# Linear attention on one core: the third pair's load of Q in pieces of 112, 10, 3 and 3 partitions, with three tiny loads between them

## The chip, the cores and the metric

The kernel runs on one core of a Trainium2 chip. The metric is the device time of one execution in microseconds (us); lower is better. Quoted for the kernel before is the median of three runs, 126.63 us (126.56 to 127.84).

## The reference

Inputs Q, K and V have the shape (8, 12, 512, 64) in float32: 96 heads of 512 rows with 64 columns. Linear attention without a mask is computed for each head:

```python
Q_feat = np.maximum(0, Q) + 1
K_feat = np.maximum(0, K) + 1
KV = np.einsum('bhkd,bhkv->bhdv', K_feat, V)
K_sum = np.sum(K_feat, axis=2)
numerator = np.einsum('bhqd,bhdv->bhqv', Q_feat, KV)
denominator = np.einsum('bhqd,bhd->bhq', Q_feat, K_sum)
return (numerator / (denominator[:, :, :, None] + 1e-10)).astype(np.float32)
```

Each of the four arrays has 12.58 MB, so 37.75 MB are read and 12.58 MB written.

## The kernel before

The 96 heads are worked on in 12 groups of eight heads (`NG` = 12), and two groups make a pair; there are six pairs, numbered 0 to 5 here, so the third is pair 2. All loads of a pair are issued together by `load_pair`: K, V and Q, each one transfer of 128 partitions, 2 MB in HBM, cast to bf16 on the way (1 MB in SBUF). They go through GpSimd's DMA queue (POOL), lines L115 (K and V) and L121 (Q). For pair 0 they are smaller pieces, and half of its Q comes through SyncE's queue (SP, L93). In a load of Q, one partition holds two runs of 32 rows of 64 columns: 16 KB of float32. Raw tiles have two buffers, so pair s+2's K can be loaded only when pair s's features have been read.

For each group the steps are:

- `k_features` and `q_features` (VectorE, L146): max(x + 1, 1) in bf16.
- `v_blocks` (VectorE L164, ScalarE L162): V of four heads is copied into a block layout `v_all` with a column of ones per block.
- `keys_values` (TensorE, L180): KV and K_sum accumulate in PSUM; ScalarE writes them to `kva_all` (L190, L191).
- `transposes` (TensorE L201, copies L204): the features of Q, transposed.
- `out_matmuls` and `norms` (TensorE L214, VectorE L231 and L232): numerator and denominator, then reciprocal and product into `o_sb`, which has three buffers.
- `store` (POOL L135 for the first ten groups, SP L138 and L141 for the last two): 1 MB of float32 to HBM.

The order on every engine is the order of the program (`manual_schedule`); each engine's queue is in order, and the framework adds the semaphores. POOL's queue holds, in this order: the loads of pairs 0, 1 and 2; then, for each later pair, K, V, Q and two stores; then the rest of the stores. The main loop issues pair 2's loads at the end of group 1, and pair 3's at the end of group 3:

```python
            if g % 2 and g // 2 + 2 < NG // 2:
                load_pair(g // 2 + 2)
            if g >= LAG:
                store(g - LAG)
```

For GpSimd's transfers the framework has eight completion semaphores, used in turn, so a transfer also waits until the eighth one before it has landed, unless that is known already. A transfer that waits holds up everything behind it in POOL's queue.

Of the kernel before, what the change touches and what calls it, by code (L numbers as in the profile page):

```python
# [8 lines left out]
FP32 = mybir.dt.float32  # L9
# [4 lines left out]
IN_BUFS = 2  # L14
OUT_BUFS = 3
LAG = 3


@with_exitstack
def kernel(  # L20
# [19 lines left out]
    nc = tc.nc  # L40

    B, H, S, D = Q.shape
    P = 128
# [10 lines left out]
    def view(t, c):  # L54
        return t.flatten_outer_dims().rearrange("(n p c) d -> p n c d", p=P, c=c)

    q_eights = view(Q, C4)
# [13 lines left out]
    psum = ctx.enter_context(tc.tile_pool(name="psum", bufs=2, space=bass.MemoryType.PSUM))  # L71
    psum_qt = ctx.enter_context(tc.tile_pool(name="psum_qt", bufs=2, space=bass.MemoryType.PSUM))

    identity = const.tile([P, P], BF16, name="identity")
    NV = 4
    v_all = const.tile([P, 2, 2, C2, 4 * D1], BF16, name="v_all")
# [7 lines left out]
    bufs = {}  # L84
# [33 lines left out]

    def load_q(s):
        t = in_pool.tile([P, 2, C4, D], BF16, name="q_raw")  # L120
        nc.gpsimd.dma_start(out=t, in_=q_eights[:, 2 * s : 2 * s + 2])  # L121
        rows = t.rearrange("p n (r c) d -> p n r c d", c=C)
        for e in range(2):
            raw["q", 2 * s + e] = [rows[:, n, :, 4 * e : 4 * e + 4] for n in range(2)]

    def load_pair(s):
        load("k", (2 * s, 2 * s + 1))
        load("v", (2 * s, 2 * s + 1))
        load_q(s)

    def store(g):
        s = g // 2
        o_to = o_dram[:, 2 * NP * s : 2 * NP * s + 2 * NP]
        if g < NG - 2:
            nc.gpsimd.dma_start(out=o_to[:, g % 2 : 2 * NP : 2], in_=outs[s][:, g % 2 : 2 * NP : 2])  # L135
            return
        if g == NG - 2:
            nc.sync.dma_start(out=o_to[:, 0 : 2 * NP : 2], in_=outs[s][:, 0 : 2 * NP : 2])  # L138
            return
        for h in range(2):  # L140
            nc.sync.dma_start(  # L141
                out=o_to[:, 2 * h + g % 2 : 2 * NP : NP], in_=outs[s][:, 2 * h + g % 2 : 2 * NP : NP]
            )
# [6 lines left out]
    def k_features(g):  # L150
        k_raw = raw.pop(("k", g))
        kf = kf_pool.tile([P, C2, 2, D], BF16, name="kf")
        for n in range(2):
            feature(kf[:, :, n], k_raw[:, n])
        kfs[g] = kf
# [12 lines left out]
    def q_features(g):  # L168
        q_raw = raw.pop(("q", g))
        qf = qf_pool.tile([P, R, C // 2, 2, D], BF16, name="qf")  # L170
        for n in range(2):
            feature(qf[:, :, :, n], q_raw[n])
        qfs[g] = qf

    def keys_values(g):
        kf = kfs.pop(g)
        kva_ps = psum_kva.tile([P, 4 * D1], FP32, name="kva_ps")
        for c in range(C2):
            for n in range(2):
                nc.tensor.matmul(  # L180
                    kva_ps[64 * n : 64 * n + 64],
                    lhsT=kf[:, c, n, :],
                    rhs=v_all[:, g % 2, n, c, :],
                    start=(c == 0),
                    stop=(c == C2 - 1),
                )
        kva = kva_diag[g % NV]
        for n in range(2):
            ps = slice(64 * n, 64 * n + 64)
            nc.scalar.copy(out=kva[ps, :, n, 0:D], in_=kva_ps[ps, 0 : 4 * D].rearrange("p (b d) -> p b d", b=4))  # L190
            nc.scalar.copy(out=kva[ps, :, n, D], in_=kva_ps[ps, 4 * D : 4 * D1])  # L191
# [49 lines left out]
    def output(g):  # L241
        for h in range(2):
            out_matmuls(g, h)
            norms(g, h)
# [11 lines left out]
    with tc.manual_schedule():  # L256
# [18 lines left out]
        for g in range(last - 1):  # L275
# [12 lines left out]
# [4 lines that stand above are left out]
        k_features(last - 1)  # L292
# [5 lines left out]
        keys_values(last - 1)  # L298
        store(last - 1 - LAG)
        q_features(last - 1)  # L300
# [8 lines left out]
        output(last)  # L309
        for g in range(last - LAG, NG):  # L310
            store(g)
# [30 lines left out]
```

## Time and profile before

| | us |
|---|---|
| median of three runs | 126.63 |
| the profiled execution's own time | 126.47 |
| its span, first to last instruction | 124.7 |
| VectorE (DVE) busy | 90.1 (72%) |
| TensorE (PE) busy | 64.2 (52%) |
| ScalarE (ACT) busy | 59.6 (48%) |
| GpSimd (POOL) busy | 26.1 (21%) |
| HBM read and written | 404 GB/s over the span |

Busy times are those of compute engines and of GpSimd's work on issuing transfers. The page also cuts the span into 40 slices of 3.1 us: a digit is the busy share of a slice in tenths, and the DMA row is the mean over the 16 DMA engines. A line of a timeline begins with the start and the duration in us; brackets at its end hold the idle time before it and what ended that. "k_raw<-in_K_dram" is a transfer from K in HBM into the tile `k_raw`.

Two kinds of records in the trace stand behind the page: packets (start, duration, size and queue of each piece that a DMA engine moves) and landings (the time of each of the 16 rises of a transfer's semaphore). They don't name the DMA engine.

### The profile page before, as it was taken

To read this page: it belongs to the slowest core of one execution; us is meant where nothing else is said; L and a number is where in the kernel's file an instruction comes from. 1 tells how busy PE (TensorE), PEld (TensorE's weight loads), DVE (VectorE), ACT (ScalarE), POOL (GpSimd) and SP (SyncE) were. 2 spreads that over 40 slices of the span, in tenths; PEclk is the share of its full clock that TensorE was granted. 3 is DMA by queue.
4 is the path that set the end of the run, shared out by engine and by line. 5 is a ranking of instruction groups with operands and counts; after the bars stand their busy time and mean duration, and the time that the engine had idled before them with its cause. 6 is when DMAs were issued, how large, how long until landed. Compare 5 with 4: busy or idle time off the path is not lost.

```text
span 124.7 us, 2349 instructions
## 1 busy us (share of the span) xinstructions
PE 64.2 (52%) x960; PEld 52.6 (42%) x960; DVE 90.1 (72%) x190; ACT 59.6 (48%) x86; POOL 26.1 (21%) x53
## 2 busy tenths in 40 slices
PE   0000874600596837939099690069394369874200
PEld 0000654600475826829088490058183158663000
DVE  4875735206999989998999950799958799969700
ACT  7505169806009981398803981603982283650000
POOL 6992020400001460207202070302020200020000
PEclk9999999995559996799855999657999855999655
DMA  3999999999999999999999999999999999999993
GB/s 89 320 212 216 206 211 212 212 215 218 206 212 212 220 213 206 212 215 217 230 406 327 210 212 219 212 342 395 230 202 215 219 247 417 419 417 415 406 409 135
DMA packets 11819, 32.13 MB, mean 258 GB/s; under 512 B 544, under 2 KB 544, under 8 KB 11680
## 3 DMA queue, kind: packets, MB, share of 16 engines
q0 software_dynamic: 10592, 28.84, 97.5%
q1 hardware_dynamic: 1216, 3.15, 6.7%
q8 instruction: 7, 0.11, 0.3%
q14 instruction: 4, 0.03, 0.1%
HBM read 37.75 MB, written 12.58 MB: 404 GB/s over the span
## 4 chain that ended last, share of the span: by engine, by line
DMA 51%; DVE 19%; PE 10%; ACT 7%; POOL 6%; issue 2%; DVEq 0%; ACTq 0%; POOLq 0%
DMA v_raw<-in_V_dram 51%; DVE o_sb L232 7%; PE kva_ps L180 7%; DVE v_all L164 7%; ACT qt L204 3%; ACT v_all L162 3%; POOL kva_all L271 2%; POOL k_raw L115 2%; DVE recip L231 2%; PE qt_ps L201 1%; PE o_ps L214 1%; POOL v_raw L115 1%; DVE qf L146 1%; DVE qt L204 1%; DVE kf L146 1%
## 5 line engine op out<-in xcount | busy, mean ns | idle before, releaser
L180 PE MATMUL kva_ps<-v_all,kf 128*64 128x260 bf16 x384 | 33.0, 343 | 16.8 <-DVE v_all L164 15.5
L214 PE MATMUL o_ps<-kva_all,qt 128*64 128x130 bf16 x384 | 19.7, 237 | 34.2 <-DVE recip L231 25.9
L164 DVE COPY v_all<-v_raw 32x2048 bf16<-32x2048 bf16 x36 | 26.1, 725 | 15.0 <-DMA v_raw<-in_V_dram 14.6
L180 PEld LDWEIGHTS <-kf 128*64 128x64 bf16 x384 | 26.6, 140 | 20.4 <-DVE v_all L164 15.9
L232 DVE TENSOR_TENSOR o_sb<-o_ps,recip 128x512 f32<-128x512 f32 x48 | 33.2, 692 | 1.6
L162 ACT COPY v_all<-v_raw 32x2048 bf16<-32x2048 bf16 x12 | 22.6, 1893 | 18.2 <-DMA v_raw<-in_V_dram 18.0
L214 PEld LDWEIGHTS <-qt 128*64 128x64 bf16 x384 | 13.7, 116 | 39.1 <-issue 23.2
L190 ACT CAST kva_all<-kva_ps 64x256 bf16<-64x256 f32 x24 | 8.9, 370 | 30.7 <-PE kva_ps L180 30.6
L204 ACT COPY qt<-qt_ps 128x1024 bf16<-128x1024 bf16 x23 | 22.2, 1015 | 2.2 <-PE qt_ps L201 1.7
L201 PE MATMUL qt_ps<-identity,qf 128*128 128x128 bf16 x192 | 14.8, 236 | 1.3 <-ACT qt L204 1.1
L135 POOL DMA_DIRECT2D out_dram<-o_sb x10 | 8.3, 830 | 32.1 <-DVE o_sb L232 27.3
L146 DVE TENSOR_SCALAR kf<-k_raw 128x1024 bf16<-128x1024 bf16 x24 | 9.5, 436 | 7.0 <-DMA k_raw<-in_K_dram 7.0
L201 PEld LDWEIGHTS <-qf 128*128 128x128 bf16 x192 | 12.6, 107 | 4.1 <-issue 1.8
L115 POOL DMA_DIRECT2D k_raw<-in_K_dram x7 | 5.4, 765 | 34.4 <-DVE kf L146 34.0
L231 DVE RECIPROCAL recip<-o_ps 128x8 f32<-128x8 f32 x48 | 9.6, 200 | 1.5 <-PE o_ps L214 1.2
L115 POOL DMA_DIRECT2D v_raw<-in_V_dram x7 | 5.4, 772 | 17.4 <-ACT v_all L162 17.4
L146 DVE TENSOR_SCALAR qf<-q_raw 128x1024 bf16<-128x1024 bf16 x22 | 8.2, 432 | 0.0
L249 DVE MEMSET v_all<- 128x2600 f32 x2 | 4.5, 2225 | 1.1 <-issue 1.1
L191 ACT CAST kva_all<-kva_ps 64x4 bf16<-64x4 f32 x24 | 4.1, 169 | 0.0
L121 POOL DMA_DIRECT2D q_raw<-in_Q_dram x5 | 3.5, 705 | 0.0
L250 ACT COPY v_all<-zero 128x1560 f32<-128x1560 f32 x2 | 2.9, 1488 | 0.0
L271 POOL MEMSET kva_all<- 128x130 bf16 x16 | 2.4, 196 | 0.0
(14 smaller groups left out, 6.6 us busy)
## 6 DMA issues: line engine op xcount, KB each, us to landing
out_dram<-o_sb POOLq DMA_DIRECT2D x10, 1024.0 KB, 25.2
k_raw<-in_K_dram POOLq DMA_DIRECT2D x5, 1024.0 KB, 21.7
v_raw<-in_V_dram POOLq DMA_DIRECT2D x5, 1024.0 KB, 21.8
q_raw<-in_Q_dram POOLq DMA_DIRECT2D x5, 1024.0 KB, 25.9
q_first<-in_Q_dram SPq DMA_DIRECT2D x1, 1024.0 KB, 4.9
k_raw<-in_K_dram POOLq DMA_DIRECT2D x2, 512.0 KB, 9.7
v_raw<-in_V_dram POOLq DMA_DIRECT2D x2, 512.0 KB, 11.4
out_dram<-o_sb SPq DMA_DIRECT2D x1, 1024.0 KB, 7.0
```

The lines of the kernel that those rows point to most:

```text
L115: nc.gpsimd.dma_start(out=bufs[x, s][:, ms], in_=drams[x][:, of])
L135: nc.gpsimd.dma_start(out=o_to[:, g % 2 : 2 * NP : 2], in_=outs[s][:, g % 2 : 2 * NP : 2])
L146: nc.vector.tensor_scalar(out=dst, in0=src, scalar1=1.0, scalar2=1.0, op0=ALU.add, op1=ALU.max)
L162: nc.scalar.copy(out=v_all[ps, g % 2, :, :, b * D : b * D + D], in_=v_raw[ps])
L164: nc.vector.tensor_copy(out=v_all[ps, g % 2, :, :, b * D : b * D + D], in_=v_raw[ps])
L180: nc.tensor.matmul(kva_ps[64 * n : 64 * n + 64], lhsT=kf[:, c, n, :], rhs=v_all[:, g % 2, n, c, :], start=(c == 0), stop=(c == C2 - 1),)
L190: nc.scalar.copy(out=kva[ps, :, n, 0:D], in_=kva_ps[ps, 0 : 4 * D].rearrange("p (b d) -> p b d", b=4))
L201: nc.tensor.transpose(qt_ps[:, c, r], qf[:, r, 2 * half + c, :, :], identity)
L204: copy(out=qts[g // 2][:, lo : lo + 2], in_=qt_ps.rearrange("p c r q -> p c q r"))
L214: nc.tensor.matmul(ops[c // 4][64 * j : 64 * j + 64, c // 2 % 2, (c % 2) * W : (c % 2) * W + W], lhsT=qt[:, c, q : q + 16, :], rhs=kva[:, ...
L231: nc.vector.reciprocal(out=recip, in_=cells[:, :, :, :, D:D1])
L232: nc.vector.tensor_tensor(out=o_sb[:, 2 * h + g % 2 : 2 * NP : NP, 4 * i : 4 * i + 4].rearrange("p n (b c) d -> p b c n d", b=2), in0=cell ...
```

## The change

Only `load_q` for pair 2 differs. Its one transfer of 128 partitions becomes four, of 112, 10, 3 and 3 partitions, which fill the same tile in order. Between them, three tiny transfers of 6, 4 and 6 partitions read two runs of 64 bytes per partition from the same part of Q into small float32 tiles of their own; nothing reads these tiles. All seven go through GpSimd's queue, in the order of `PIECES`. The bytes that the kernel needs and all compute instructions are the same.

```diff
+SPLIT = 2
+PIECES = ((112, True), (10, True), (6, False), (3, True), (4, False), (3, True), (6, False))
...
+    skip_pool = ctx.enter_context(tc.tile_pool(name="skip_pool", bufs=1))
+    skips = []
...
     def load_q(s):
         t = in_pool.tile([P, 2, C4, D], BF16, name="q_raw")
-        nc.gpsimd.dma_start(out=t, in_=q_eights[:, 2 * s : 2 * s + 2])
+        if s == SPLIT:
+            lo = 0
+            for n, real in PIECES:
+                if real:
+                    nc.gpsimd.dma_start(
+                        out=t[lo : lo + n], in_=q_eights[lo : lo + n, 2 * s : 2 * s + 2]
+                    )
+                    lo += n
+                else:
+                    skip = skip_pool.tile([8, 2, 16], FP32, name=f"skip{len(skips)}")
+                    skips.append(skip)
+                    nc.gpsimd.dma_start(
+                        out=skip[0:n], in_=q_eights[0:n, 2 * s : 2 * s + 2, 0, 0:16]
+                    )
+            assert lo == P
+        else:
+            nc.gpsimd.dma_start(out=t, in_=q_eights[:, 2 * s : 2 * s + 2])
```

## The prediction

> **What bounds the kernel now.** I read the page from the top: the 40 slices, the DMA queues, the chain that ended last. Then came POOL's waits, POOL's and VectorE's timelines around the change, and last the landing records of the trace (each transfer raises its semaphore 16 times, once per DMA engine).
>
> The page, slices, queues, chain:
>
> ```profile
> PE   0000874600596837939099690069394369874200
> DVE  4875735206999989998999950799958799969700
> DMA  3999999999999999999999999999999999999993
> GB/s 89 320 212 216 206 211 212 212 215 218 206 212 212 220 213 206 212 215 217 230 406 327 210 212 219 212 342 395 230 202 215 219 247 417 419 417 415 406 409 135
> ...
> q0 software_dynamic: 10592, 28.84, 97.5%
> q8 instruction: 7, 0.11, 0.3%
> q14 instruction: 4, 0.03, 0.1%
> ...
> DMA 51%; DVE 19%; PE 10%; ACT 7%; POOL 6%; issue 2%; DVEq 0%; ACTq 0%; POOLq 0%
> ```
>
> The DMA row is at 9 from the second slice to the last but one, while PE and DVE have holes. GB/s counts bytes written: near 212 is a load that reads float32 and writes bf16, near 415 a store. From slice 33 (102 us) on there are stores alone, still at full rate. So what sets the end is how many bytes each of the 16 DMA engines has to move, and which engine finishes last. The chain view ends in DVE's last multiply, but that store finds a queue in front of it: the last store is issued at 117.6 us and lands at 123.81.
>
> The landing records say how even the 16 are. For the last store they are 122.10, 122.11, 122.28, 122.64, 122.67, 122.86, then 123.09, 123.19, 123.24, 123.25, then 123.32, 123.33, 123.34, 123.35, 123.46 and 123.81. The mean is 123.00: the last engine is 0.81 us behind it. The spread is not there at the start: the second load of V lands within 0.56 us (17.65 to 18.21). It grows by one engine at a time after each 16 KB packet of the instruction queue q8 (25.9, 44.7, 55.6 us and so on, 0.9 us each): at 28 us one engine is 0.84 behind the next, at 62 us three are. So engines that also carry instructions are late, and stay late.
>
> POOL's timeline and waits, where the third pair (pair 2) and the next are issued:
>
> ```profile
> 22.54 0.70 POOL L121 DMA_DIRECT2D q_raw<-in_Q_dram  x1
> 37.10 0.77 POOL L115 DMA_DIRECT2D k_raw<-in_K_dram  x1 [13.86 <-DVE kf L146]
> 42.36 0.82 POOL L115 DMA_DIRECT2D v_raw<-in_V_dram  x1 [4.49 <-ACT v_all L162]
> 43.17 0.70 POOL L121 DMA_DIRECT2D q_raw<-in_Q_dram  x1
> 43.85 1.80 POOL L135 DMA_DIRECT2D out_dram<-o_sb  x2
> 51.94 0.75 POOL L115 DMA_DIRECT2D k_raw<-in_K_dram  x1 [6.28 <-DVE kf L146]
> ```
>
> The first line is the transfer that is cut up. It is issued at 22.54 and lands at 48.86: 26 us in the queue. POOL itself idles 13.86 us before its next transfer.
>
> **The change, part by part.**
>
> *One load becomes four; rows move between engines.* 128 rows on 16 engines are 8 each. A row of pair 2's Q is 16 KB of float32; V before it lands at 42.74 on the mean of the engines and Q at 47.72, so 8 rows take 4.98 us and one row 0.62. In the change 112 rows give 7 to each engine, if spread evenly, and 16 rows in pieces of 10, 3 and 3 are left, which no longer fall one on each engine. Where they fall the trace can't show, since it has no transfer of fewer than 128 rows; so bounds. Best: the six engines that are early at the end get two of these rows, the four in the middle one, the six late ones none. The early end at 122.86 + 0.62 = 123.48 at the latest, the middle at 123.25, the late at 123.81 - 0.62 = 123.19; the end moves from 123.81 to 123.48, or -0.33. Worst: the latest engine itself has one row more (+0.62), or two more (+1.23). Two readings can be counted out, engines numbered 0 to 15. If each small transfer begins at the engine where the last one stopped, one row each, the pieces fall on 0-9, 0-2 and 7-9 and the tiny loads on the gaps: 6 engines get an extra row, 4 none, and 6 lose one. If each begins at the same engine, three engines get two extra rows. I take the first and its best end, because 6, 4 and 6 are also the groups of the sorted landings; the order of the engines within them is taken on trust.
>
> The Trainium skill (DMA: Bandwidth & Descriptors, "Why a DMA increments its semaphore by 16 and not by 1") states the first reading for GpSimd transfers whose count has no larger share: k consecutive engines from a cursor that moves on. It also has an exception, measured for some direct copies, in which the rows fill the engines from 0. The sum is -0.33 by the one and up to +1.23 by the other; no run here shows either yet.
>
> *Six more transfers in the queue.* Each ends in one 4-byte semaphore packet on every engine, 22 ns in the packet records: 6 x 22 = +0.13 us on each engine, all of it on the bound. They could be had for 9 ns (the records' least): +0.05.
>
> *The tiny loads.* 6 + 4 + 6 rows with two runs of 64 bytes are 32 packets, two per engine if spread. The nearest rows are the 4-byte packet (9 to 22 ns) below and the 2 KB packet of a store (84 ns) above: 0.02 to 0.17 us. 64 bytes are nearer to 4: I take 0.05. A page of the skill speaks against all of this (same page, "Measured", its rule and fit): a GpSimd DMA has about 2.0 us fixed, and transfers under 64 KB are mostly overhead. The trace disagrees for queued transfers: landings are 4.9 to 5.0 us apart for one load after another, which is the packets' own time (a load of K is 32 packets per engine, 154 ns apart: 4.93). By the rule six transfers would be +12 us; by the row they are the +0.13 above.
>
> *POOL's time.* Six more issues at 0.70 us (the Q line above; the smallest, for half the bytes, is 0.57) are 4.2 us. They fall into the 13.86 us of idle before the next K, so nothing; without that cover it would be 4.2 us of later issues, and again only as far as the queue runs out.
>
> *New waits on POOL.* In the built program a GpSimd transfer waits for the eighth one before it, and six small ones bring this closer. The first three-row piece waits for pair 1's K (landed 23.16), the skip of 4 for its V (29.03), the second three-row piece for its Q (33.89), the last skip for pair 2's K (38.84). All are queued before the 112 rows are through (about 48). Behind them stands pair 3: K now waits for pair 2's V, 43.84 instead of 37.10; V for the 112 rows, about 48.2 instead of 42.36; Q and two stores follow until about 51.5, and the next K is issued at 51.94 anyway. Does the queue run dry? The earliest engine is through pair 2's Q at 47.24 in the old trace. From issue to first packet the trace gives only an upper bound: the very first K is issued at 1.29 and starts at 4.93, behind the first Q, so at most 3.64. 43.9 + 3.64 = 47.5 is 0.3 us past that engine, which in the change is one with more rows, through at 47.9. For V: 48.2 + 3.64 = 51.8, before K is through (52.2). So nothing, and at the bound 0.3.
>
> *VectorE* now waits for four semaphores before the Q features of pair 2. They start late anyway:
>
> ```profile
> 48.94 0.69 DVE L232 TENSOR_TENSOR o_sb<-o_ps,recip 128x512 f32<-128x512 f32 x1
> 49.55 0.75 DVE L146 TENSOR_SCALAR qf<-q_raw 128x1024 bf16<-128x1024 bf16 x2
> ```
>
> 49.55 against a landing at 48.86: 0.69 us of cover. Without it a late row would push DVE, the transposes and the stores of that pair, which wait in the same deep queue.
>
> **The sum.** Against the profiled execution: 126.47 us, of which 124.70 are span and 1.77 lie around it. -0.33 + 0.13 + 0.05 = -0.15, so 126.32. The median of the three runs is 126.63, 0.16 above the profiled execution; -0.15 from it is 126.48, and I say 126.5.
>
> **The rivals.**
>
> *The rows fall on the wrong engines* (the slower side). Place: the engine that lands last at 123.81. Price: +0.62 for one row more, +1.23 for two, and 0.18 for packets: 127.4 or 128.0. It decides as soon as the latest engine has nine rows; over 1% it is only with ten. For it: the trace names no engine. Against it: the counts 6, 4, 6. Chance 0.16.
>
> *The rows spread evenly*, the pieces being cut over all 16 engines: then nothing is balanced and only packets are left, 126.63 + 0.18 = 126.8. Against it: three rows are six runs, which 16 engines can't share evenly. Chance 0.12.
>
> *The queue runs dry* behind POOL's later waits. Place: pair 3's K, with 3.3 us between its issue and the end of pair 2's Q instead of 10. Price: each us it starts past 47.9 is a us at the end. At the bound for the start 0.3: 126.8; if the tiny loads land late, some 2 us and 128.5. For it: POOL has no idle left there. Against it: every wait has landed before the 112 rows. Chance 0.07.
>
> *More than balancing*: perfect balance gives 123.00, -0.81, so 126.0 with the packets. Over 1% faster needs a gain that no row shows. Chance 0.10, half of it over 1%.
>
> **How the numbers follow.** The forecast keeps 0.55; its own range is 126.2 (markers free) to 126.9 (upper prices of the tiny loads and of a 0.3 us gap). Within 1% (125.4 to 127.9), about what a measurement of this kernel can tell from no change, lie the forecast, the even spread, one row too many and most of the balanced case. Slower by over 1%: two rows on the latest engine (about half of the first rival) and the dry queue, with some room for a price that I missed: 0.17. Faster by over 1%: 0.08. The range to hold it 8 times in 10 goes from full balance to one row on the wrong engine: 125.9 to 127.6.
>
> **What would show it.** Right: the last store's landings lie within 1.0 us instead of 1.71, the last near 123.7; pair 3's K is issued near 44 and V near 48; the DMA row stays at 9; the Q features of pair 2 still start near 49.5. Wrong: one engine lands over 0.5 us behind the next at the end (wrong rows), a slice near 48 to 54 us drops below 9 (dry queue), or the spread is unchanged (no rows moved). A time beyond 127.6 or below 125.9 means that a step of the sum is missing.

## The result and the profile after

| | before | after |
|---|---|---|
| median, us | 126.55 (6 runs) | 128.03 (6 runs) |
| the profiled execution's own time, us | 126.47 | 128.83 |
| span, us | 124.7 | 127.0 |
| last landing of the last store, mean of the 16 engines, us | 123.00 | 124.30 |
| the same, last engine, us | 123.81 | 126.14 |

The ratio is 1.0113 (95% interval 1.0075 to 1.0151): the change makes the kernel slower, by 1.5 us of 126.6. The prediction was 126.5 with a range of 125.9 to 127.6, so it was wrong in size and in sign. (The slowest of the six runs is left out of the ratio: its state differs from the others'.)

In all 14 profiles of this case the execution's own time is 2.65 to 2.69 us more than the last landing of the last store. So two things make up the time: when the 16 engines are through on the mean (1.30 us later after the change), and how far the last engine is behind that mean (0.81 us before, 1.84 after).

The page after. Again the DMA and GB/s rows in 40 slices, the queues, and the chain:

```profile
DMA  3999999999999999999999999999999999999991
GB/s 88 328 209 213 210 208 211 217 209 217 208 211 213 221 186 170 197 213 221 219 408 323 197 210 216 219 341 388 228 214 213 217 294 414 418 417 412 406 353 62
...
q0 software_dynamic: 10800, 28.84, 96.5%
...
DMA 56%; DVE 20%; ACT 7%; PE 7%; issue 2%; POOL 1%; ACTq 0%; POOLq 0%
```

The DMA row is still at 9, so by that row nothing happened. The row below tells it: slices 15 to 17 (44 to 54 us) move 186, 170 and 197 GB/s where the kernel before moved 213, 206 and 212. Packets became longer there (an example follows below) and count as busy for all of their length, so the share stays up while the bytes fall.

The same as a table by stretches: busy time of each engine, then PE's clock, DMA share and GB/s. First two stretches of before, then after:

```profile
core 0: us, PE busy (x) PEld busy (x) DVE busy (x) ACT busy (x) POOL busy (x), PEclk, DMA share, GB/s
47.00:50.00 3.00, 2.41 (x32) 2.01 (x34) 2.90 (x9) 0.16 (x1) 0.00 (x0) 0.66 1.08 205
50.00:53.00 3.00, 3.00 (x46) 2.46 (x44) 2.99 (x7) 1.11 (x5) 0.75 (x1) 0.78 1.12 210
```

```profile
44.00:47.00 3.00, 0.27 (x9) 0.23 (x7) 2.87 (x7) 2.50 (x5) 1.16 (x1) 0.89 1.05 209
47.00:50.00 3.00, 2.90 (x38) 2.37 (x36) 2.52 (x6) 0.00 (x0) 1.18 (x2) 0.54 1.03 159
50.00:53.00 3.00, 2.37 (x48) 1.90 (x42) 2.99 (x8) 2.12 (x6) 2.48 (x4) 1.00 1.10 190
53.00:56.00 3.00, 0.42 (x8) 0.28 (x8) 2.89 (x6) 2.58 (x2) 0.38 (x2) 1.00 1.12 210
```

The missing bytes, (205 - 159) x 3 + (210 - 190) x 3 = 198 KB, are 0.93 us at 212 GB/s. The landings say the same. On the mean of the 16 engines, pair 3's K lands 9.93 us after pair 2's V before and 11.02 us after, and pair 3's Q 19.85 and 21.06 us after that V. What a kernel takes longer than 19.85 us for this last stretch is called its loss below: 1.21 us for the changed kernel, -0.01 in a second profile of the kernel before.

What happens there is seen in POOL's timeline (start, duration, then the transfer; in brackets the idle time and what ended it):

```profile
22.53 1.27 POOL L129 DMA_DIRECT2D q_raw<-in_Q_dram  x2
23.79 0.57 POOL L136 DMA_DIRECT2D skip<-in_Q_dram  x1
24.34 0.57 POOL L129 DMA_DIRECT2D q_raw<-in_Q_dram  x1
28.95 0.60 POOL L136 DMA_DIRECT2D skip<-in_Q_dram  x1 [4.04 <-DMA v_raw<-in_V_dram]
33.84 0.55 POOL L129 DMA_DIRECT2D q_raw<-in_Q_dram  x1 [4.28 <-DMA q_raw<-in_Q_dram]
38.80 0.55 POOL L136 DMA_DIRECT2D skip<-in_Q_dram  x1 [4.41 <-DMA k_raw<-in_K_dram]
44.05 1.16 POOL L119 DMA_DIRECT2D k_raw<-in_K_dram  x1 [4.70 <-DMA v_raw<-in_V_dram]
48.82 0.76 POOL L119 DMA_DIRECT2D v_raw<-in_V_dram  x1 [3.61 <-DVE recip L251]
```

The last three of the seven pieces and tiny loads each wait for the eighth transfer before, one landing after another, and so do the next two loads: pair 3's K is issued at 44.05 instead of 37.10, its V at 48.82 instead of 42.36. (The last line names DVE; the eighth transfer before that V is the piece of 112 rows, which lands at 48.24.) The first packets of that K start at 47.16 us, right behind pair 2's Q, so no gap shows at first sight. But between 47.3 and 47.8 us six packets of K last 1.09 to 1.23 us, where the same packet in a running queue lasts 0.17. That the engines had nothing read ahead is how I read this; the records don't show the reading side.

### The profile page after: what moved, and what is told of

It is laid out like the page before. It is cut to its first block, busy times and chain, and to the rows that moved or that the text cites. A ratio compares the mean times of both kernels' runs of the same rounds, so it can differ in the third digit from the quotient of the medians.

```text
span 127.0 us, 2358 instructions
## 1 busy us (share of the span) xinstructions
PE 65.8 (52%) x960; PEld 53.9 (42%) x960; DVE 89.8 (71%) x190; ACT 59.6 (47%) x86; POOL 30.2 (24%) x59
## 4 chain that ended last, share of the span: by engine, by line
DMA 56%; DVE 20%; ACT 7%; PE 7%; issue 2%; POOL 1%; ACTq 0%; POOLq 0%
DMA v_raw<-in_V_dram 56%; DVE v_all L184 8%; DVE o_sb L252 8%; PE kva_ps L200 6%; ACT qt L224 3%; ACT v_all L182 3%; DVE recip L251 2%; ACT kva_all L210 1%; DVE qf L166 1%; DVE qt L224 1%; POOL k_raw L119 1%; DVE kf L166 1%; PE o_ps L234 1%; PE qt_ps L221 0%; ACT kva_all L211 0%
## 5 line engine op out<-in xcount | busy, mean ns | idle before, releaser
L184 DVE COPY v_all<-v_raw 32x2048 bf16<-32x2048 bf16 x36 | 25.4, 707 | 15.5 <-DMA v_raw<-in_V_dram 15.1
L221 PE MATMUL qt_ps<-identity,qf 128*128 128x128 bf16 x192 | 16.2, 249 | 0.7 <-ACT qt L224 0.4
L221 PEld LDWEIGHTS <-qf 128*128 128x128 bf16 x192 | 13.7, 113 | 3.4 <-issue 1.4
L136 POOL DMA_DIRECT2D skip<-in_Q_dram x3 | 1.7, 574 | 8.4 <-DMA k_raw<-in_K_dram 4.4
L129 POOL DMA_DIRECT2D q_raw<-in_Q_dram x4 | 2.4, 599 | 4.3 <-DMA q_raw<-in_Q_dram 4.3
```

What stands on the lines that cost most here:

```text
L184: nc.vector.tensor_copy(out=v_all[ps, g % 2, :, :, b * D : b * D + D], in_=v_raw[ps])
L221: nc.tensor.transpose(qt_ps[:, c, r], qf[:, r, 2 * half + c, :, :], identity)
```

## The experiments

Three theories. **W**: the later issue of pair 3's loads lets the DMA queue run dry, fully or nearly. **P**: each small transfer has a price of its own on every engine (the landings of the small transfers of the changed kernel are 0.18 to 0.20 us apart). **R**: the rows went to engines that were late anyway (the last landings of the changed kernel spread over 3.31 us instead of 1.71).

### More and more tiny loads, no row moved

Pair 2's Q stays whole; 4, 5, 6 or 8 tiny loads of 16 partitions follow it (the list is written short here). The number decides what pair 3's K must wait for.

```diff
-PIECES = ((112, True), (10, True), (6, False), (3, True), (4, False), (3, True), (6, False))
+PIECES = ((128, True),) + ((16, False),) * n      # n = 4, 5, 6, 8
```

n = 4: 

> Pair 2's Q is one transfer of 128 partitions again, followed by four tiny loads of 16 partitions each. No row moves, and with four extra transfers pair 3's K waits for pair 1's Q (landed 34), so it is still issued at about 37. Theory W (the later waits on POOL let the DMA queue run dry): no loss, mean landing as before within 0.15 us, time within 0.3 us of before. Theory P (each small transfer costs about 0.19 us on every engine, as the landings of the changed kernel are apart): mean of the landings up by 4 x 0.19 = 0.76, time +0.7 us. Theory R (only the rows on wrong engines cost): no loss.

n = 5: 

> Pair 2's Q whole, then five tiny loads of 16 partitions: pair 3's K waits for pair 2's K, issued near 39.5, V near 44.4, Q near 49. Theory W: all of these are still more than 4 us ahead of the queue's end, so no loss between 47 and 53 us, time 126.5 to 127.1. If the loss grows with the number of transfers: between the kernel with four (126.95) and the one with six (128.85), about 127.9.

n = 6: 

> The same with six tiny loads of 16 partitions: no row moves, but pair 3's K now waits for pair 2's V and is issued at about 44, V at about 48, as in the changed kernel. Theory W: pair 3's K starts cold, its first packets on the early engines take about 1.1 us, the engines lose about 0.6 to 0.9 us between 47 and 53 us, time +0.7 to +1.0 us. Theory P: 6 x 0.19 = +1.1 us, only 0.4 more than with four. Theory R: within 0.3 us of before.

n = 8: 

> Pair 2's Q whole, then eight tiny loads of 16 partitions. The last tiny load now waits for that Q (landed at about 48.5), and pair 3's K for the first tiny load, so K is issued near 50, when the queue is empty. Theory W: first packet about 3.1 us after the issue and about 1 us more until it runs at rate, so all engines stand still from 48.5 to about 53: 4 to 5.5 us lost on each engine, time 130.5 to 132.5. If instead six or more extra transfers have some fixed price: about 129.

| n | issue of pair 3's K, of its V, us | loss, us | median, us | ratio (interval) |
|---|---|---|---|---|
| before | 37.1, 42.4 | 0 | 126.6 | |
| 4 | 37.2, 41.6 | 0.06 | 126.95 | 1.0024 (1.0009 to 1.0038) |
| 5 | 39.6, 44.6 | 0.33 | 126.99 | 1.0029 (1.0001 to 1.0057) |
| 6 | 44.7, 50.3 | 1.38 | 128.85 | 1.0180 (1.0143 to 1.0217) |
| 8 | 49.8, 50.7 | 5.88 | 132.74 | 1.0470 (1.0428 to 1.0512) |

The issues with n = 5, then with n = 6 (the first of these lines names DVE; the transfer that K waits for, pair 2's K, lands at 39.01):

```profile
39.56 0.79 POOL L119 DMA_DIRECT2D k_raw<-in_K_dram  x1 [4.72 <-DVE recip L251]
44.59 1.13 POOL L119 DMA_DIRECT2D v_raw<-in_V_dram  x1 [4.24 <-ACT qt L224]
```

```profile
44.74 1.16 POOL L119 DMA_DIRECT2D k_raw<-in_K_dram  x1 [4.73 <-DMA v_raw<-in_V_dram]
50.26 0.92 POOL L119 DMA_DIRECT2D v_raw<-in_V_dram  x1 [4.36 <-DMA q_raw<-in_Q_dram]
```

The steps are not those of a price per transfer: in the median the fifth costs nothing and the sixth about 1.9 us, as W says. W had the place right but priced it low: 0.7 to 1.0 us were expected for n = 6, and it is 2.3; for n = 8 132.74 us is just above the 132.5 expected at most. The landings of the tiny loads are 0.18 to 0.19 us apart here too, yet with four of them pair 3's K lands 5.00 us after pair 2's Q, against 4.95 before: a small transfer delays its own semaphore, hardly the bytes behind it. P falls. The 0.3 to 0.4 us of n = 4 and n = 5 are in part unevenness: the mean of the last landings is 123.04 and 123.15, against 123.00 and 123.07 in two profiles of the kernel before, but the last engine is 1.23 and 1.01 us behind that mean, against 0.81 and 1.23. Whether the extra transfers make this is not shown. The spread of the last landings is 3.11 us with n = 6, though no row was moved: a wide spread is no sign of R.

With eight the queue is empty, and the page shows what a start costs. Its DMA and GB/s rows, and POOL's timeline:

```profile
DMA  3999999999999953999999999999999999999991
GB/s 105 302 212 212 211 209 210 212 217 210 212 213 214 217 101 27 194 212 214 210 197 412 280 212 212 220 239 413 294 213 214 214 236 402 421 416 415 406 398 76
```

```profile
49.27 0.51 POOL L136 DMA_DIRECT2D skip<-in_Q_dram  x1 [4.34 <-DMA skip<-in_Q_dram]
49.78 0.89 POOL L119 DMA_DIRECT2D k_raw<-in_K_dram  x1
50.67 0.86 POOL L119 DMA_DIRECT2D v_raw<-in_V_dram  x1
```

K is issued at 49.78 and its first packet starts at 51.38. From 52.5 to 53.0 us the queue moves 131 GB/s, from 53.0 to 53.5 it moves 205. From issue to full rate that is about 3.2 us.

### The same waits and transfers, even rows

```diff
+PIECES = ((112, True), (16, True)) + ((16, False),) * 5
```

> 112 partitions, the other 16 in one piece, five tiny loads of 16: the same seven transfers and the same waits on POOL as in the changed kernel (K at 44, V at 48.8), but each engine has eight rows. Theory W: the dry queue is there, 0.7 to 1.0 us lost on each engine between 47 and 53 us, time 127.5 to 128.3. Theory R: 126.6 to 126.9.

128.96 us, ratio 1.0171 (1.0130 to 1.0211), loss 1.72 us. The rows are even and the whole slowdown is there, more of it than the 128.3 expected at most. R is not needed for it.

### The same rows, without the late issue

The third tiny load is moved behind pair 3's Q:

```diff
+PIECES = ((112, True), (10, True), (6, False), (3, True), (4, False), (3, True))
...
+            if s == SPLIT + 1:
+                skip = skip_pool.tile([16, 2, 16], FP32, name="skip_last")
+                nc.gpsimd.dma_start(out=skip[0:6], in_=q_eights[0:6, 2 * s : 2 * s + 2, 0, 0:16])
```

> The four pieces and the first two tiny loads as in the changed kernel, so the rows lie the same; the third tiny load is issued behind pair 3's Q. With five extra transfers ahead of it, pair 3's K waits for pair 2's K (39) and V for pair 2's V (44.4) instead of 44 and 48.8. Theory W (POOL's late issue lets the DMA queue run dry): the loss between 47 and 53 us is gone (under 0.1 us an engine), mean of the last landings within 0.3 us of before, time 126.3 to 127.2. Theory R (the rows): spread of the last landings about 3.3 us as in the changed kernel, time 127.3 or more. If the rows balance as intended and W holds: spread under 1.3 us, 126.2.

POOL's timeline of this kernel:

```profile
39.45 0.78 POOL L119 DMA_DIRECT2D k_raw<-in_K_dram  x1 [4.68 <-DVE recip L254]
44.47 1.14 POOL L119 DMA_DIRECT2D v_raw<-in_V_dram  x1 [4.24 <-DMA v_raw<-in_V_dram]
49.13 0.70 POOL L141 DMA_DIRECT2D q_raw<-in_Q_dram  x1 [3.53 <-DMA q_raw<-in_Q_dram]
```

127.09 us, ratio 1.0030 (1.0005 to 1.0054), loss 0.21. One tiny load moved by three places takes back about 1 us of the 1.5. The last landings spread over 2.06 us. Five extra transfers with whole rows, which are issued at the same times, have the ratio 1.0029: against them the rows, as they lie in the change, show no cost, and against the kernel before at most the 0.5 us. They gain nothing.

### Where the rows fall

> The pieces of 112, 10, 3 and 3 partitions without the tiny loads: three extra transfers, no later issue of pair 3's K. If small transfers go on at the engine where the last one stopped, 10 + 3 + 3 cover the 16 engines once and the rows are even: last landings spread by 1.7 us as before, time +0.1 (W, R) or +0.5 us (P). If each small transfer begins at the same engine, three engines get two rows more: spread 2.5 us or more, time +0.6 to +1.2 us.

> Pieces of 112 and 10, a tiny load of 6, a piece of 6: three extra transfers, no later issue of pair 3's K. If transfers go on where the last one stopped, six engines get one row more, six one less, four none, as in the changed kernel though not all the same engines. Theory R: spread of the last landings 2.3 to 3.3 us and time +0.4 to +1.2 us if the rows go to engines that are late, less than 1.3 us and -0.3 if they go to early ones. Theories W and P: spread near 1.7 us; W time within 0.3 us of before, P +0.5 us.

> The mirror of the kernel with a 6-partition piece behind a tiny load of 6: 112, tiny 6, 10, tiny 10, 6. If small transfers go on where the last one stopped, the six engines that lost a row there get one here. Four extra transfers, no later issue of pair 3's K. If the late engines are a fixed set and rows matter, one of the two mirrors is slower than before and the other not: the sum of their differences to before is near zero, each within 0.6 us. Theory W alone: both within 0.3 us of before.

```diff
+PIECES = ((112, True), (10, True), (3, True), (3, True))                              # first
+PIECES = ((112, True), (10, True), (6, False), (6, True))                             # second
+PIECES = ((112, True), (6, False), (10, True), (10, False), (6, True))                # third
```

126.68 us, ratio 1.0000 (0.9979 to 1.0021); 126.79 us, 1.0025 (0.9999 to 1.0051); 127.16 us, 1.0041 (1.0023 to 1.0060). None loses anything in the queue (0.04, 0.04, 0.05 us). The first keeps the engines nearly as they were: the standard deviation of their landings goes from 0.52 us (pair 2's V) to 0.64 (pair 3's K); with five tiny loads and whole rows it goes from 0.37 to 0.45. In the second it goes from 0.58 to 0.72, in the third from 0.39 to 0.73, and in the kernel of the section before from 0.33 to 0.62, with groups near -0.7, -0.35 and +0.4 us and one engine at +1.63. The third and the last fit the reading that a small transfer goes on at the engine where the last one stopped; the second, which should show it too, hardly does (rows that fall on early engines would hide it). The Trainium skill (DMA: Bandwidth & Descriptors, "Why a DMA increments its semaphore by 16 and not by 1") states that a GpSimd transfer of k shares, with k under 16, takes k consecutive engines from a round-robin cursor. The records name no engine, so this stays open. The spreads of the last landings are 2.43, 3.28 and 2.83 us, and no run shows what the rows have in that. The two mirrors (the second and third) were expected to differ in sign if the late engines were a fixed set. They don't: neither is faster.

> The kernel before once more, for a second profile: if the order in which the engines finish is fixed, the last landings lie as in the first (six early, four in the middle, six late, spread 1.7 us); if it changes from execution to execution, the groups and the spread differ.

126.96 us in one run. The last landings, as differences from their mean of 123.07: -1.13, -0.81, -0.74, -0.41, -0.36, -0.30, -0.26, -0.21, -0.19, 0.25, 0.33, 0.40, 0.41, 0.65, 1.14, 1.23. The spread is 2.36 us instead of 1.71, and there are no groups of 6, 4 and 6. How uneven the engines are differs between two executions of one program.

### The late issue alone

This is the kernel before, without a piece or a tiny load: POOL copies two elements per partition out of each of the two tiles whose landing pair 3's K and V wait for in the changed kernel.

```diff
+    def late(name, src):
+        t = late_pool.tile([P, 2], BF16, name=name)
+        nc.gpsimd.tensor_copy(out=t, in_=src)
...
     def load_pair(s):
+        if s == 3:
+            late("late_k", bufs["v", 2][:, 0, 0, 0:2])
         load("k", (2 * s, 2 * s + 1))
+        if s == 3:
+            late("late_v", raw["q", 4][0][:, 0, 0, 0:2])
         load("v", (2 * s, 2 * s + 1))
```

> The kernel before with no extra transfer and no piece: POOL copies two elements of pair 2's V ahead of pair 3's K, and two elements of pair 2's Q ahead of pair 3's V, so these loads are issued when V and Q have landed (about 44.4 and 49), as in the changed kernel. Theory W (only the late issue counts): 0.9 to 1.5 us lost on each engine between 46 and 60 us, time 127.5 to 129.0. Theory R or a price of the extra transfers: within 0.3 us of before, 126.3 to 126.9.

Its POOL timeline and two of its stretches:

```profile
43.97 0.70 POOL L129 COPY late_k<-v_raw 128x2 bf16<-128x2 bf16 x1 [20.82 <-DMA v_raw<-in_V_dram]
44.62 1.02 POOL L116 DMA_DIRECT2D k_raw<-in_K_dram  x1
48.85 0.18 POOL L129 COPY late_v<-q_raw 128x2 bf16<-128x2 bf16 x1 [3.21 <-DVE o_sb L241]
49.36 0.74 POOL L116 DMA_DIRECT2D v_raw<-in_V_dram  x1 [0.33 <-issue]
```

```profile
47.00:50.00 3.00, 2.66 (x32) 2.17 (x34) 2.90 (x8) 0.00 (x0) 0.82 (x2) 0.51 1.00 154
50.00:53.00 3.00, 2.95 (x52) 2.40 (x48) 3.00 (x7) 1.54 (x5) 3.00 (x5) 0.92 1.07 184
```

128.86 us, ratio 1.0147 (1.0113 to 1.0181), loss 1.71 us. The same two stretches have the same hole (159 and 190 in the changed kernel). The late issue alone, with the transfers and rows of the kernel before, is enough for the whole slowdown. W stands. The spread of the last landings is 3.12 us here, again without a moved row; most of it is one engine, 2.29 us behind the next, so the profiled execution took 130.15 us.

### The changed kernel again

> The changed kernel once more, for a second profile. Theory W: again first packets of pair 3's K that take about 1 us on several engines near 47.5 us, and 0.8 to 1.1 us lost on each engine between 46 and 56 us. The spread of the last landings need not be 3.3 us again, since the order of the engines differed between two profiles of the kernel before.

128.51 us in one run. K is issued at 44.63 and V at 49.61, and the loss is 1.55 us. Packets of K last 0.56 to 0.89 us near 48, and of V up to 1.56 us near 52.3 to 53.2. The spread of the last landings is 2.51 us instead of 3.31.

## Why the prediction was wrong, point by point

- **What bounds the kernel** was right: the bytes through the DMA queue. In every kernel here the median loses what the queue loses, and up to 0.9 us more; how far the last engine falls behind the mean has its part in that.
- **New waits on POOL** is the step that failed: "So nothing, and at the bound 0.3." The waits themselves came nearly as worked out: K at 43.9 was 44.05, V at 48.2 was 48.82. K and V are issued about 0.55 us after the last engine's landing (V of pair 2 lands at 43.49, K is issued at 44.05), which was not in the sum. The error was the test put to them. I asked whether the first packet could *start* before the queue ran out, and it does (47.16, behind a lead of 3.1 us). But a queue is fed only when its next transfer runs at full rate, and that took about 3.2 us from the issue with an empty queue. Take as lead the time from the issue to the end of the work queued ahead, on the earliest engine. With a lead of 7.3 to 7.4 us (five extra transfers) pair 3's K lands 0.1 to 0.2 us later than before; with 2.3 to 3.1 it lands 0.2 to 1.2 later. V shows the limit better: with a lead of 3.8 us (the late issue alone) or 4.0 (the changed kernel) it lands 5.06 and 4.97 us after K, as before (5.00); with 2.8 to 3.0 (six tiny loads, even rows, the changed kernel again) 5.58 to 5.75. The profiled loss is 1.21 us, against nothing in the sum. The bound of 3.64 us was taken on a first packet that stood behind another queue's transfer, and I used it as if it held for the rate.
- **The rival "The queue runs dry"** named the right place, pair 3's K, and priced it at 126.8 to 128.5. 128.03 lies in it, in part by luck: 126.8 was its price at the bound for the start, and 128.5 stood for tiny loads that land late, which they did not. It got a chance of 0.07, because of the step above. A lead that falls from 10 us to 3, with the only number for a start at 3.64, deserved several times that.
- **One load becomes four, rows move**: -0.33 was taken. Measured without the late issue it is no gain, and +0.5 us at most (127.09 against 126.59), which five tiny loads with whole rows cost nearly as well. The six, four and six of the sorted landings are not there in the second profile. Reading a pattern of 0.6 us out of one execution, and then trusting that the engines behind it are a fixed set, was the second error.
- **Six more transfers in the queue, the tiny loads**: +0.18 was taken; with four tiny loads behind a whole Q, K lands 0.06 us later, with five 0.12. Right in that they are cheap. The packets were counted wrongly: the tiny loads of the change are 16 packets of 128 bytes (one per partition, 0.013 us each) and not 32, and GpSimd's queue carries 160 more packets of 4 bytes and 32 of 8, where 96 of 4 bytes were in the sum.
- **POOL's time** for the issues: hidden, as said; six issues of 0.55 to 0.60 us.
- **VectorE**: predicted to start pair 2's Q features near 49.5 with no wait. They start at 49.67 after 0.41 us of waiting, which is not where the time went:

```profile
48.57 0.69 DVE L252 TENSOR_TENSOR o_sb<-o_ps,recip 128x512 f32<-128x512 f32 x1
49.67 1.18 DVE L166 TENSOR_SCALAR qf<-q_raw 128x1024 bf16<-128x1024 bf16 x3 [0.41 <-DMA q_raw<-in_Q_dram]
```

- **What would show it**: "the DMA row stays at 9" was put down as right and "a slice drops below 9" as a dry queue. Neither could see a loss of 1.2 us; GB/s did. (With eight tiny loads, where the queue was empty, the DMA row fell to 5 and 3.) "One engine over 0.5 us behind the next", put down as wrong rows, came too (125.23 to 125.88 us), but the late issue alone has such a gap without a moved row.

Left open: the profiled execution of the changed kernel has a second, smaller hole at 71 us (four packets of about 1 us), which the kernel before has once at 90 us; why the changed kernel loses a little less than those with even rows or with the late issue alone (1.0113 against 1.0147 to 1.0180, the intervals touch); the 0.3 us of four or five tiny loads; and why the engines end up uneven. No kernel tried beats the one before.

## What to carry to other kernels

A small transfer added to an in-order queue with a fixed number of completion semaphores cost next to nothing by itself here, but it moves every later wait of that queue; count which landing the next large load now waits for, and how long before the end of the queued work that is. Ask for a lead that covers the way to full rate (here about 3.2 us; 3.0 us were too short for V and 3.8 enough), not for one that covers the first packet. And before work is moved between engines by their order in one profile, a second profile of the same program should show that order again.

## What was not expected of the hardware

- The DMA row can hide a starving queue: behind the late issue, 2 KB packets took up to 1.23 us instead of 0.17, and the row stayed at 9 where GB/s was 170, against 206 in the kernel before.
- The landings of small queued transfers are 0.18 to 0.20 us apart, though four of them delayed the load behind them by 0.06 us only.
- After the last landing that POOL waited for, loads of K and V were issued 0.54 to 0.58 us later, loads of Q, small pieces and tiny loads 0.28 to 0.29.
